# Convolution: sixteen of its 120 multiply-add taps made on the scalar engine and summed by accumulating DMA, two after each head norm

## The chip, the cores and the metric

The kernel runs on one NeuronCore of a Trainium2 chip. The metric is device time in microseconds (us) of that core. Five engines work side by side, each through its own instructions in order: PE (TensorE, matrix products), DVE (VectorE), ACT (ScalarE), POOL (GpSimd) and SP (SyncE, which here only issues DMAs). POOL also issues DMAs, among them those that add to their target while they write it ("accumulating" DMAs).

## What is computed

Two transformer-like blocks run on one sequence of 512 tokens with 1024 channels, all in float32. The change lies in the first half of the second block:

```python
proj = rms_norm(x, norm1_g) @ w_in
q, k, v, glu_a, glu_b = split(proj)            # 512 columns each
q = rms_norm(q per head of 64, q_norm_g);  k = rms_norm(k per head, k_norm_g)
attn = stick_breaking_attention(q, k, v)       # 8 heads, strictly causal
c = glu_a * sigmoid(glu_b)
c = causal_depthwise_conv(c, conv_dw_w, conv_dw_b)   # 31 taps, 512 channels
c = silu(layer_norm(c, conv_ln_g, conv_ln_b))
x = x + concat([attn, c]) @ w_out
```

The depthwise convolution is a sum over k of `w[k] * c[t - 30 + k]`, for each channel on its own. Everything else (the first block, the two feed-forward parts) stays as it is.

## The kernel before

Activations stand with channels in the partitions: a row of 512 channels is four chunks of 128 partitions x 512 tokens. A product in near-float32 is made of three PE passes (`mm3`, lines 127 to 129), each on a high or a low part of the operands; `copy_split` (L135, L136) and `scale_split` (L143, L144) make these parts, the high one on ACT and the low one on DVE.

Weights come in units of 1 MB through `prep`: SP loads `raw`, ACT casts it to `whi` (L199), and the low part `wlo` is made either by DVE (L205) or, for the eight units in `SUMMED`, by ACT writing minus the high part (L202) and POOL issuing an accumulating DMA that adds `raw` to it (L203). `raw`, `whi` and `wlo` have two buffers each.

The stage that matters runs so. `glu(i)` (four of them) makes chunk i of the gated input into `cc`. `heads` runs twice, for q and for k; for each of four token tiles it makes 24 PE products into one PSUM tile, squares it on ACT (L742), sums by head on DVE (L744), makes the reciprocal root on POOL in three small instructions (L745 to L747) and multiplies on DVE (L748, here called the head norm's last step). Then PE transposes the four tiles (L755, 16 products on the identity) and `scale_split` makes qT or kT. `project` makes v. The attention goes over twelve steps (hp, n) with hp 0 to 3 and n 0 to 2: `sticks` makes scores on PE (L785, L790), takes their absolute value on ACT for hp 0 and 1 (L794) and on DVE for hp 2 and 3 (L797), exp and ln on ACT (L799, L800), the sum on DVE (L801) and its two parts (L135, L136); `breaks` adds the tail sums on PE (L814, L817) and takes exp on ACT (L819); `gather` makes the weighted sum on PE (L829).

The convolution lies in between. `conv(n, after)` emits the next n taps of the list `TURNS`, each one DVE instruction `cv[:, i] += w[k] * cc[:, i, k:k+512]` (L851); the first tap of a chunk stands on an ACT instruction with scale and bias (L132). All 120 taps are chained by `issue_after`, so that they stay in order. When the last is done `conv_norm` makes the layer norm (L889 to L917). `attended` and `half_out` are the products with w_out.

A scheduler puts the emitted instructions into each engine's order by its own estimate of times; an engine then waits at each instruction for what that needs, and everything queued behind waits too.

Of the kernel before, what the change touches and what calls it, by code (L numbers as in the profile page):

```python
# [10 lines left out]
F32 = mybir.dt.float32  # L11
F32R = mybir.dt.float32r
I32 = mybir.dt.int32
AF = mybir.ActivationFunctionType
ALU = mybir.AluOpType
# [3 lines left out]
T = 512  # L19
# [60 lines left out]
def block_kernel(  # L80
# [12 lines left out]
    pe, act, dve, pool, sp = nc.tensor, nc.scalar, nc.vector, nc.gpsimd, nc.sync  # L93
# [78 lines left out]
    def half(name, a, b, dt=F32R):  # L172
        return part(slot(name, dt), a, b)
# [77 lines left out]
    def par(name, i=0, n=1):  # L251
        o = _SMALL[name][0] + i
        return sm[:, o : o + n]
# [119 lines left out]
    for u in range(2):  # L373
# [10 lines left out]
        sums = {}  # L384
# [307 lines left out]
    cc = part(ht[0], 4, 544)  # L692
    cv = part(ht[1], 4, T)
# [3 lines left out]
    def glu(i):  # L697
        pt = sta_unit(ph, pl)
        if i == 0:
            norms()  # L700
        ab = v3(t4(), 2, 512)
        dve.tensor_tensor(ab, pt, over2(rb2), ALU.mult)
        sig = act.activation(ab[:, 1, :], ab[:, 1, :], AF.Sigmoid)
        if i == 3:
            with tc.issue_after(sig.ins):
                act.preload_act_table_set(tables)
        return dve.tensor_tensor(cc[:, i, 30:542], ab[:, 0, :], ab[:, 1, :], ALU.mult)  # L707
# [18 lines left out]
    rr, rr2 = keep("rr"), keep("rr2")  # L726

    def heads(name, gain, sc, taps, between, early=()):

        gc = col(1)  # L730
        dve.tensor_scalar(gc, par(gain), sc, None, ALU.mult)
        ws = list(early) + [weights() for _ in range(2 - len(early))]
        dst = [half(name + "0", 4, T), half(name + "1", 4, T)]
        for t in range(NT):
            ps = single() if t < 2 else pair()[:, 0, :]
            st = slice(t * P, (t + 1) * P)
            for k in range(KC):
                wh, wl = (w[:, k % 4, :] for w in ws[k // 4])
                mm3(ps, ph[:, k, st], pl[:, k, st], wh, wl, k == 0, k == KC - 1)
            qn = norm2[:, t, :]  # L740
            heads8 = qn.rearrange("p (b d) -> p b d", d=HD)
            act.activation(qn, ps, AF.Square)  # L742
            ms = tp.tile([P, 8], F32, tag="col16", name="col16", bufs=6)
            dve.tensor_reduce(ms, heads8, AX.X, ALU.add)  # L744
            pool.tensor_scalar(ms, ms, rr2[:, t : t + 1], EPS, ALU.mult, ALU.add)  # L745
            pool.tensor_tensor(ms, ms, mhalf[:, :8], ALU.pow)  # L746
            pool.tensor_scalar(ms, ms, rr[:, t : t + 1], None, ALU.mult)  # L747
            conv(taps[t], dve.tensor_tensor(heads8, ps.rearrange("p (b d) -> p b d", d=HD),  # L748
                                            ms.unsqueeze(2).to_broadcast([P, 8, HD]), ALU.mult))
        between()  # L750
        for i in range(2):
            tr = pair().rearrange("p a (b c) -> p (a b) c", b=2)
            for t in range(2):
                for hp in range(4):
                    pe.transpose(tr[:, hp, t * P : (t + 1) * P],  # L755
                                 norm2[:, 2 * i + t, hp * P : (hp + 1) * P], ident)
            ts = slice(2 * i * P, (2 * i + 2) * P)
            scale_split(dst[0][:, :, ts], dst[1][:, :, ts], tr, gc)
        return dst
# [72 lines left out]

    TURNS = [0] * 8 + [0, 1] * 22 + [1, 2] * 8 + [2, 3] * 22 + [3] * 8
    done = [0] * 4
    tap = None

    def conv(n, after=None):

        nonlocal tap
        tap = after or tap
        for _ in range(min(n, len(TURNS))):
            i = TURNS.pop(0)
            k = done[i]
            done[i] += 1
            if k == 0:
                identity(cv[:, i, :], cc[:, i, 30:542], scale=par("dw_w", 4 * 30 + i),
                         bias=par("dw_b", i))
            with tc.issue_after(tap.ins) if tap else nullcontext():  # L850
                tap = dve.scalar_tensor_tensor(  # L851
                    cv[:, i, :], cc[:, i, k : k + 512], par("dw_w", 4 * k + i), cv[:, i, :],
                    ALU.mult, ALU.add)

    norm2 = half("D1", 4, T, F32)
    conv(8, glu(0))
    split_early(2)
    conv(16, glu(1))
    qT = heads("G", "qg", HD ** -0.5, (0, 4, 4, 8), lambda: conv(8, glu(2)), early[:2])
    kT = heads("F", "kg", 1.0, (0, 6, 5, 8), lambda: conv(12, glu(3)), early[2:])  # L860
    v2 = half("E0", 4, T, F32)
    stk = {}

    def place(i):
# [106 lines left out]
    seq = [(hp, n) for hp in range(4) for n in range(3)]  # L971
# [4 lines left out]
    todo = 2  # L976
    for i, x in enumerate(seq):

        while todo < len(seq) and todo <= i + 2 and not (x[1] == 2 and seq[todo][1] == 1):
            conv(2, sticks(*seq[todo]))  # L980
            todo += 1
        weighted = breaks(*x)
        if x[1] == 2:
            gathered = gather(x[0])
    with tc.issue_after(weighted.ins):
        act.preload_act_table_set("silu_and_others")
    assert not TURNS
    conv_norm()
# [127 lines left out]
```

## Time and profile before

| | us |
|---|---|
| median of 3 runs (lowest, highest) | 1244.39 (1243.74, 1244.77) |
| the profiled execution | 1245.94 |
| its span, first to last instruction | 1244.2 |
| mean granted TensorE clock in it | 0.995 of full |
| PE busy | 1230.3 (99%) |
| DVE busy | 754.0 (61%) |
| ACT busy | 495.0 (40%) |
| POOL busy | 113.5 (9%) |

Times below count from the first instruction of the profiled execution. Busy time of PE is modelled (products overlap), so that a busy PE is not always a PE at its peak; the distance from one product's start to the next's, and the waits, are the better measure. The second block starts near 665 us; the last attention product starts near 841 us.

### The profile page before, as it was taken

The page shows a single profiled execution, that of the slowest core. Times are in us where ns is not written, and L with a number is a line of the kernel's source. Part 1 is how long each engine was busy: PE and PEld are TensorE (multiplying, and loading weights), DVE is VectorE, ACT ScalarE, POOL GpSimd, SP SyncE. Part 2 cuts the span into 40 slices and gives each one's busy share as a digit, 9 for nine tenths or more (in the row PEclk, how much of TensorE's full clock was granted, in tenths as well). Part 3 has the DMA queues.
Part 4 walks back from the last instruction along what each step waited for, and adds up shares of the span by engine and source line. Part 5 has one row for each costly group of instructions (what it writes and reads, how often), then busy time and mean ns, then how long its engine had stood idle before and what let it go on. Part 6 is the DMA issues. An engine that isn't in the chain of part 4 may idle for free.

```text
span 1244.2 us, 13667 instructions
## 1 busy us (share of the span) xinstructions
PE 1230.3 (99%) x5712; PEld 1014.1 (82%) x5712; DVE 754.0 (61%) x823; ACT 495.0 (40%) x534; POOL 113.5 (9%) x137
## 2 busy tenths in 40 slices
PE   9999999999999999999999999999999999999998
PEld 7889888788888888888888887667888888888887
DVE  7855634744766674466373899877575555346532
ACT  6433424623544342243255338764343333123310
POOL 1100210012000000000053440000400000000000
PEclk9999999999999999999999999899999999999999
DMA  7223222312222222222346254301322222222222
GB/s 274 101 104 132 102 102 68 136 68 98 73 100 102 102 102 102 88 85 99 119 152 169 68 130 104 106 1 68 102 102 82 89 100 102 102 102 102 84 70 83
DMA packets 21597, 126.71 MB, mean 102 GB/s; under 512 B 2336, under 2 KB 4256, under 8 KB 7840
## 3 DMA queue, kind: packets, MB, share of 16 engines
q1 hardware_dynamic: 20096, 117.20, 26.7%
q0 software_dynamic: 1152, 8.39, 3.5%
q8 instruction: 44, 0.72, 0.2%
q10 hardware_dynamic: 288, 0.26, 0.1%
q14 instruction: 17, 0.14, 0.0%
HBM read 115.35 MB, written 2.10 MB: 94 GB/s over the span
## 4 chain that ended last, share of the span: by engine, by line
PE 90%; DVE 4%; POOL 2%; ACT 2%; issue 1%; DMA 1%; SPq 0%; DVEq 0%; POOLq 0%; ACTq 0%
PE pp L129 27%; PE pp L127 27%; PE pp L128 27%; DVE H L851 2%; PE ps L128 1%; PE ps L129 1%; PE ps L127 1%; POOL col L746 1%; PE pp L814 1%; PE pp L817 1%; PE ps L829 1%; DMA wlo<-raw 1%; POOL col L745 1%; PE pp L785 0%; PE ps L326 0%
## 5 line engine op out<-in xcount | busy, mean ns | idle before, releaser
L199 ACT CAST whi<-raw 128x2048 fp32r<-128x2048 f32 (+3 forms) x109 | 197.9, 1817 | 415.5 <-PE pp L128 335.7
L129 PE MATMUL pp<-B,wlo 128*128 128x512 f32 x672 | 262.5, 391 | 0.2
L127 PE MATMUL pp<-B,whi 128*128 128x512 f32 x672 | 261.7, 390 | 0.8 <-ACT whi L199 0.7
L128 PE MATMUL pp<-C,whi 128*128 128x512 f32 x672 | 262.2, 390 | 0.0
L205 DVE TENSOR_TENSOR wlo<-raw,whi 128x2048 fp32r<-128x2048 f32 (+3 forms) x101 | 219.3, 2172 | 66.1 <-ACT whi L199 65.6
L128 PE MATMUL pp<-G,whi 128*128 128x512 f32 x448 | 175.0, 391 | 0.0
L129 PE MATMUL pp<-F,wlo 128*128 128x512 f32 x416 | 162.2, 390 | 0.0
L127 PE MATMUL pp<-F,whi 128*128 128x512 f32 x416 | 161.5, 389 | 0.0
L129 PEld LDWEIGHTS pp<-B,wlo 128*128 128x128 f32 x672 | 126.1, 188 | 28.2 <-DVE wlo L205 1.5
L127 PEld LDWEIGHTS pp<-B,whi 128*128 128x128 f32 x672 | 126.3, 188 | 28.0 <-ACT whi L199 1.7
L128 PEld LDWEIGHTS pp<-C,whi 128*128 128x128 f32 x672 | 126.2, 188 | 26.8 <-issue 0.5
L128 PEld LDWEIGHTS pp<-G,whi 128*128 128x128 f32 x448 | 84.1, 188 | 17.5 <-issue 0.2
L655 DVE SCALAR_TENSOR_TENSOR H<-H,sm,H 128x512 f32<-128x512 f32 x132 | 92.8, 746 | 0.7
L634 DVE TENSOR_TENSOR A<-pp,A 128x1024 f32<-128x1024 f32 x23 | 28.2, 1224 | 105.5 <-PE pp L129 105.5
L129 PEld LDWEIGHTS pp<-F,wlo 128*128 128x128 f32 x416 | 78.1, 188 | 16.5 <-issue 0.2
L127 PEld LDWEIGHTS pp<-F,whi 128*128 128x128 f32 x416 | 78.1, 188 | 16.4 <-issue 0.2
L851 DVE SCALAR_TENSOR_TENSOR H<-H,sm,H 128x512 f32<-128x512 f32 x120 | 83.2, 742 | 2.7 <-ACT H L132 2.5
L660 DVE TENSOR_TENSOR H<-pp,rb 128x1024 f32<-128x1024 f32 x22 | 26.8, 1224 | 50.6 <-PE pp L129 44.4
L132 ACT ACTIVATE H<-H,sm 128x512 f32<-128x512 f32 x70 | 54.3, 808 | 4.6 <-DVE H L707 4.6
L1010 DVE TENSOR_TENSOR H<-pp,rb 128x512 f32<-128x512 f32 x22 | 15.2, 691 | 60.4 <-PE pp L129 55.3
L127 PE MATMUL pp<-D,whi 128*128 128x512 f32 x112 | 43.6, 389 | 0.0
L128 PE MATMUL pp<-E,whi 128*128 128x512 f32 x112 | 43.6, 389 | 0.0
(315 smaller groups left out, 1826.3 us busy)
## 6 DMA issues: line engine op xcount, KB each, us to landing
raw<-in_wts SPq DMA_DIRECT2D x99, 1024.0 KB, 4.8
wlo<-raw POOLq DMA_DIRECT2D x8, 1024.0 KB, 7.0
raw<-in_wts SPq DMA_DIRECT2D x8, 768.0 KB, 4.2
A<-in_xT SPq DMA_DIRECT2D x3, 512.0 KB, 6.7
out<-A SPq DMA_DIRECT2D x3, 512.0 KB, 2.8
D<-in_memT SPq DMA_DIRECT2D x1, 1024.0 KB, 11.4
raw<-in_wts SPq DMA_DIRECT2D x3, 256.0 KB, 7.6
A<-in_xT SPq DMA_DIRECT2D x2, 256.0 KB, 3.9
```

What stands on the lines that cost most here:

```text
L127: pe.matmul(out, wh, xh, start=start, stop=False, **kw)
L128: pe.matmul(out, wh, xl, start=False, stop=False, **kw)
L129: pe.matmul(out, wl, xh, start=False, stop=stop, **kw)
L132: act.activation(out, in_, AF.Identity, scale=scale, bias=bias)
L199: act.copy(hi[:, cs], raw[:, cs])
L205: dve.tensor_tensor(lo[:, cs], raw[:, cs], hi[:, cs].bitcast(F32), ALU.subtract)
L634: dve.tensor_tensor(hu, pt, hu, ALU.add)
L655: dve.scalar_tensor_tensor(dst, hs[:, k : k + 512], w(k), dst, ALU.mult, ALU.add)
L660: dve.tensor_tensor(hs[:, :, 2:], pt, over2(rb), ALU.mult)
L745: pool.tensor_scalar(ms, ms, rr2[:, t : t + 1], EPS, ALU.mult, ALU.add)
L851: tap = dve.scalar_tensor_tensor(cv[:, i, :], cc[:, i, k : k + 512], par("dw_w", 4 * k + i), cv[:, i, :], ALU.mult, ALU.add)
L1010: dve.tensor_tensor(hs[:, 2:514], pt[:, 0, :], rb, ALU.mult)
```

## The change

Taps 22 to 29 of chunks 0 and 1 leave `TURNS` (16 of 120). In their place `by_dma`, called once behind each of the eight head norms, makes two products `w[k] * cc[:, i, k:k+512]` on ACT (i = 0 and 1). For the first tap (k = 22) they are written straight into `sums[:, 0:2]`; for the other seven, into `sums[:, 2:4]`, from where POOL issues an accumulating DMA (256 KB) into `sums[:, 0:2]`, not before the last POOL instruction of that head norm (`power`, L747). That is 16 products and 14 DMAs. After the k heads one DVE instruction (128 x 1024) adds the sums to chunks 0 and 1 of `cv`. `sums` lies in the buffer D0, which the first attention step writes next. `TURNS` is reordered, and in the attention loop each step now emits one tap where it emitted two.

```diff
-            pool.tensor_scalar(ms, ms, rr[:, t : t + 1], None, ALU.mult)
+            power = pool.tensor_scalar(ms, ms, rr[:, t : t + 1], None, ALU.mult)
             conv(taps[t], dve.tensor_tensor(heads8, ps.rearrange("p (b d) -> p b d", d=HD),
                                             ms.unsqueeze(2).to_broadcast([P, 8, HD]), ALU.mult))
+            by_dma(power)
...
-    TURNS = [0] * 8 + [0, 1] * 22 + [1, 2] * 8 + [2, 3] * 22 + [3] * 8
+    TURNS = [0] * 8 + [0, 1] * 14 + [1] * 8 + [2] * 26 + [2, 3] * 4 + [3] * 26
...
+    sums = half("D0", 4, T, F32)
+    aside = list(range(22, 30))
+
+    def by_dma(behind):
+        k = aside.pop(0)
+        for i in range(2):
+            out = sums[:, i, :] if k == 22 else sums[:, 2 + i, :]
+            act.activation(out, cc[:, i, k : k + 512], AF.Copy, scale=par("dw_w", 4 * k + i))
+            if k > 22:
+                with tc.issue_after(behind.ins):
+                    pool.dma_start(out=sums[:, i, :], in_=out, accum_op=ALU.add)
+
     conv(8, glu(0))
...
     v2 = half("E0", 4, T, F32)
+    dve.tensor_tensor(cv[:, 0:2, :], cv[:, 0:2, :], sums[:, 0:2, :], ALU.add)
...
-            conv(2, sticks(*seq[todo]))
+            conv(1, sticks(*seq[todo]))
```

The scheduler's orders change with it, at three places above all. In each fence the words in brackets name the engines or DMA lanes that the instruction waits for (lanes of POOL's DMAs are DMASW, of SP's DMAHW).

POOL, from the third tile of the k heads to the fourth, before:

```order
L745 TENSOR_SCALAR col_4896<-col_4896,rr_4358 128x8 [waits DVE_49]
L746 TENSOR_TENSOR col_4896<-col_4896,mhalf 128x8 [waits Pool_49]
L747 TENSOR_SCALAR col_4896<-col_4896,rr 128x8 [waits Pool_49]
L203 DMA wlo<-raw 128x2048 [waits DMAHW3_49,DMASW2_49,Activation_49]
L745 TENSOR_SCALAR col_4933<-col_4933,rr_4358 128x8 [waits DVE_49]
L746 TENSOR_TENSOR col_4933<-col_4933,mhalf 128x8 [waits Pool_49]
L747 TENSOR_SCALAR col_4933<-col_4933,rr 128x8 [waits Pool_49]
```

and now:

```order
L868 DMA D_4360<-D_4360 128x512 [waits DMASW2_49,Activation_49]
L868 DMA D_4360<-D_4360 128x512 [waits DMASW3_49,Activation_49]
L745 TENSOR_SCALAR col_4919<-col_4919,rr_4358 128x8 [waits DVE_49]
L746 TENSOR_TENSOR col_4919<-col_4919,mhalf 128x8 [waits Pool_49]
L747 TENSOR_SCALAR col_4919<-col_4919,rr 128x8 [waits Pool_49]
L868 DMA D_4360<-D_4360 128x512 [waits DMASW4_49,Activation_49]
L868 DMA D_4360<-D_4360 128x512 [waits DMASW5_49,Activation_49]
L203 DMA wlo<-raw 128x2048 [waits DMAHW3_49,Activation_49]
L745 TENSOR_SCALAR col_4960<-col_4960,rr_4358 128x8 [waits DVE_49]
L746 TENSOR_TENSOR col_4960<-col_4960,mhalf 128x8 [waits Pool_49]
L747 TENSOR_SCALAR col_4960<-col_4960,rr 128x8 [waits Pool_49]
```

Two DMA issues, each waiting for an ACT product, now stand ahead of each head norm's three instructions, and ahead of the weight's DMA (L203).

ACT at the same place (L742 squares a tile, L202 and L199 prepare a unit of v's weights), before:

```order
L742 ACTIVATE D_4359<-pp 128x512 [waits PE_49]
L202 ACTIVATE wlo<-raw 128x2048 [waits DMAHW3_49,DMASW2_49,PE_49]
L742 ACTIVATE D_4359<-pp 128x512 [waits PE_49,Activation_49]
L199 CAST whi<-raw 128x2048
L199 CAST whi<-raw 128x2048 [waits DMAHW4_49,PE_49,Activation_49]
```

and now:

```order
L865 ACTIVATE D_4360<-H_2137,sm 128x512 [waits DMASW2_49,Activation_49]
L865 ACTIVATE D_4360<-H_2137,sm 128x512 [waits DMASW3_49,Activation_49]
L742 ACTIVATE D_4359<-pp 128x512 [waits PE_49]
L865 ACTIVATE D_4360<-H_2137,sm 128x512 [waits DMASW4_49,Activation_49]
L865 ACTIVATE D_4360<-H_2137,sm 128x512 [waits DMASW5_49,Activation_49]
L202 ACTIVATE wlo<-raw 128x2048 [waits DMAHW3_49,PE_49]
L742 ACTIVATE D_4359<-pp 128x512 [waits PE_49]
L199 CAST whi<-raw 128x2048
L865 ACTIVATE D_4360<-H_2137,sm 128x512 [waits DMASW6_49,Activation_49]
L865 ACTIVATE D_4360<-H_2137,sm 128x512 [waits DMASW7_49,Activation_49]
```

Each product waits until the DMA of the tap before has read and summed its buffer, and the squares of the head norm and the weight casts stand behind it in ACT's order.

PE, where the scores of the first attention steps (L785, L790) stand among v's products (the 128x512 rows onto `ps`; the first that reads the second unit's `wlo` is the last row shown), before:

```order
L785 MATMUL pp<-G_4552,F_4798 128x384 x2
L790 MATMUL pp<-never,identr 128x128 x2
L785 MATMUL pp<-G_4552,F_4798 128x256 x2
L785 MATMUL pp<-G_4552,F_4798 128x128 x2
L790 MATMUL pp<-never,identr 128x128 x4
L785 MATMUL pp<-G_4552,F_4797 128x512 x2
L785 MATMUL pp<-G_4553,F_4797 128x512 x2
L128 MATMUL ps_5124<-wlo,B_4163 128x512
```

and now:

```order
L786 MATMUL pp<-G_4553,F_4813 128x384 x2
L786 MATMUL pp<-G_4554,F_4813 128x384 x2
L786 MATMUL pp<-G_4553,F_4814 128x384 x2
L791 MATMUL pp<-never,identr 128x128 x2
L128 MATMUL ps_5156<-wlo,B_4163 128x512
```

Twelve score rows that stood ahead of that product now stand behind it. The last score rows of step (0, 2) now stand behind all of v's products, right ahead of the first tail sums:

```order
L128 MATMUL ps_5234<-wlo,B_4163 128x512
L129 MATMUL ps_5234<-whi,C_4165 128x512
L786 MATMUL pp<-G_4553,F_4814 128x512 x2
L791 MATMUL pp<-never,identr 128x128 x2
L815 MATMUL pp<-D_5098,negone 128x128 x2
```

Before, the same four rows stood 48 of v's products earlier, so that ACT could begin with step (0, 2) there. In the changed kernel DVE and PE also reach `conv_norm` inside the attention loop instead of behind it.

## Rows read from the trace of the kernel before

**Rows 1.** Busy time by stretch: us, then each engine's busy us, PEclk, DMA share, GB/s.
```profile
712.00:746.00 34.00, 34.00 (x159) 28.28 (x158) 32.27 (x48) 12.61 (x13) 15.56 (x14) 1.00 0.45 113
746.00:780.00 34.00, 33.87 (x179) 26.93 (x176) 33.97 (x47) 27.88 (x29) 2.65 (x3) 1.00 0.47 115
780.00:836.00 56.00, 50.27 (x300) 35.95 (x300) 44.10 (x56) 36.89 (x47) 0.00 (x0) 0.91 0.17 51
...
789.30:799.50 10.20, 9.34 (x45) 8.05 (x45) 7.70 (x9) 5.82 (x8) 0.00 (x0) 0.50 0.04 18
```

**Rows 2.** PE's longer waits from 780 to 862: total us, times, longest.
```profile
PE ps L829 <- ACT C L819: 1.5, 1, 1.5
PE ps L829 <- ACT E L819: 0.9, 1, 0.9
PE pp L785 <- ACT C L819: 0.9, 1, 0.9
PE pp L814 <- DVE t L801: 0.9, 1, 0.9
PE pp L814 <- DVE B L136: 0.7, 1, 0.7
PE pp L127 <- DVE A L957: 0.7, 1, 0.7
```

**Rows 3.** Timeline of DVE in the second attention step: start, us, instruction, idle before.
```profile
789.37 0.96 DVE L801 SCALAR_TENSOR_TENSOR t<-pp,t 128x768 f32<-128x768 f32 x1
```

**Rows 4.** Timeline of ACT just before it, same columns.
```profile
788.49 0.85 ACT L800 ACTIVATE t<-t 128x768 f32<-128x768 f32 x1
```

**Rows 5.** Timeline of DVE: eight taps in a row, and one 128x1024 step.
```profile
706.39 5.38 DVE L851 SCALAR_TENSOR_TENSOR H<-H,sm,H 128x512 f32<-128x512 f32 x8
...
746.52 1.21 DVE L702 TENSOR_TENSOR t<-pp,rb 128x1024 f32<-128x1024 f32 x1
```

**Rows 6.** Timeline of ACT: a 128x512 scaling, and a weight step in the k heads.
```profile
686.38 0.80 ACT L132 ACTIVATE H<-H,sm 128x512 f32<-128x512 f32 x1
...
733.64 1.92 ACT L202 ACTIVATE wlo<-raw 128x2048 fp32r<-128x2048 f32 x1 [4.62 <-PE pp L128]
```

**Rows 7.** Timeline of POOL: the fourth k tile's norm and two weight DMA issues.
```profile
735.86 0.93 POOL L203 DMA_DIRECT2D wlo<-raw  x1 [0.53 <-ACT wlo L202]
738.74 1.27 POOL L745 TENSOR_SCALAR col<-col,rr 128x8 f32<-128x8 f32 x1 [1.95 <-DVE col L744]
740.09 2.06 POOL L746 TENSOR_TENSOR col<-col,mhalf 128x8 f32<-128x8 f32 x1
742.25 0.31 POOL L747 TENSOR_SCALAR col<-col,rr 128x8 f32<-128x8 f32 x1
748.60 0.94 POOL L203 DMA_DIRECT2D wlo<-raw  x1 [6.04 <-ACT wlo L202]
```

**Rows 8.** Timeline of DVE: the last step of the fourth k tile's norm.
```profile
742.60 0.69 DVE L748 TENSOR_TENSOR D<-pp,col 128x512 f32<-128x512 f32 x1 [0.66 <-POOL col L747]
```

**Rows 9.** DMA queue of POOL (packets, MB, share), and issues (count, KB, us to landing).
```profile
q0 software_dynamic: 1152, 8.39, 3.5%
...
wlo<-raw POOLq DMA_DIRECT2D x8, 1024.0 KB, 7.0
...
A<-in_xT SPq DMA_DIRECT2D x2, 256.0 KB, 3.9
```

**Rows 10.** Timeline of PE: transposes of k, first scores, a product on v's second unit.
```profile
744.55 1.91 PE L755 MATMUL pp<-ident,D 128*128 128x128 f32 x16
...
746.53 0.40 PE L128 MATMUL ps<-wlo,B 128*128 128x512 f32 x1
...
752.30 1.26 PE L785 MATMUL pp<-G,F 64*128 64x256 f32 x14
...
755.68 0.50 PE L128 MATMUL ps<-wlo,B 128*128 128x512 f32 x1
```

**Rows 11.** Timeline of ACT: the absolute value of step (0, 2).
```profile
763.00 1.01 ACT L794 ACTIVATE t<-pp 128x1024 f32<-128x1024 f32 x1
```

## The prediction

> **What bounds the kernel now.** I read busy time by stretch first [rows 1]. From 712 to 780 us, where the heads of q and k and v's products run, PE is busy for 67.87 of 68 us: nothing that shortens DVE there shortens the kernel. DVE is as full (66.24 of 68), so it looks like a bottleneck, but nobody who ends the time waits for it. PE has idle time only in the attention loop: 5.73 of 56 us between 780 and 836. There the second view, PE's waits, says for whom [rows 2]: 1.6 us for DVE (L801 0.9, L136 0.7), the rest, 4.1 us, for ACT, above all for the exp (L819) between two PE products that depend on each other. One more wait for DVE (L957, 0.7) lies behind the loop. The third loss is the clock: from 789.3 to 799.5 PE was granted 0.50, the lower of its two levels (1.2 of 2.4 GHz), right behind the first cluster of waits. It was busy 9.34 us of that [rows 1], so at the full clock the same work takes 4.7 us less. All that a better convolution can win is thus about 1.6 + 0.7 us of waits for DVE and, if the waits go far enough, 4.7 us of clock.
>
> **What the taps cost.** Eight taps in a row take 5.38 us, start to start 0.66 [rows 5]; sixteen fewer free 10.6 us of DVE, and the one 128x1024 addition takes about 1.2 back (the same shape, L702, took 1.21 [rows 5]): 9.4 us net. On PE's path that is worth little. The wait for L801 ended at 789.37 + 0.96, and L801 started at 789.37, 0.03 us after the ln that it needs (788.49 + 0.85) [rows 3, 4]: the two taps ahead of it held it up by nothing. I leave 0 for the two waits in the loop and take the 0.7 of L957, since the layer norm's DVE work moves out of that place into the loop. Bounds: 0 and 2.3 us won. **Gain 0.7.**
>
> **What the products cost.** Sixteen at about 0.74 (the 128x512 scaling took 0.80 with its end [rows 6]) are 12 us of ACT, in a stretch where ACT is busy 12.61 of 34 us [rows 1]: room enough, as work. What counts is order: the squares (L742) and v's weight casts stand behind products that wait for a landing.
>
> **The landing** of a 256 KB accumulating DMA is not in the trace. The 1 MB ones land 7.0 us after their issue [rows 9]. Their queue shows 3.5% of 16 engines' 1244 us, 697 us for 8 DMAs: 5.4 us per engine and DMA. With a quarter of the bytes in as many packets this is 1.4 if bytes decide and 5.4 if packets do, so the landing lies between 1.6 + 1.4 = 3.0 and 7.0 us. A plain 256 KB load of the same shape took 3.9, in the crowded start [rows 9]. I take 3.2, near the end by bytes. The Trainium skill ("DMA: Bandwidth & Descriptors", section "Anatomy of one DMA — SWDGE (gpsimd) path") gives 2.0 us plus bytes over 436 GB/s, an estimate of 2.6 us here, and by it the sum below would be +2.6 instead of +3.0; but for 1 MB it gives 4.4 where the trace shows 7.0, so the trace decides.
>
> **POOL and the k heads.** An issue takes 0.93 and a norm 1.27 + 2.06 + 0.31 = 3.64 [rows 7], so a tile now costs POOL 2 x 0.93 + 3.64 = 5.5 us. PE makes a tile in the same time: 25 products lie between 746.53 and 752.30 [rows 10], 0.23 each, 24 to a tile. POOL can follow, but works off no lag. The first two products stand ahead of the first square and leave a lag of about 1.2; two issues add 1.86. So the weight issue (L203) behind the third k norm goes from 735.86 to about 738.9, the fourth norm ends near 739.9 + 3.64 = 743.5, and its last DVE step (L748, 0.69) near 744.3 instead of 743.3 [rows 7, 8]. The transposes start at 744.55, and those that need the fourth tile half of 1.91 later, at 745.4 [rows 10]: 1.1 us of lead are left. **Cost 0** at 3.2. If the landing is longer, each tile's chain is landing + 0.74, against 5.5: it is covered up to 4.7, and at 7.0 three tiles lose 2.2 each, 6.6 us, less the lead: 5.5 on PE. The q heads have more room, their second half of transposes moved nine products back.
>
> **v's weights.** The low part of v's first unit is now issued at about 738.9; with 7.0 us [rows 9] it lands at 745.9, and PE reads it at 746.53 [rows 10]; since small DMAs are still in flight on that queue I take a wait of 0.4. The second unit's issue stays near 748.60 [rows 7], because its cast waits for PE, not for the products; it lands at 755.6. Before, 28 score rows stood ahead of the product that reads it, and PE came to it at 755.68 [rows 10]. Now sixteen do, so that PE is there at about 752.30 + 28 rows' 3.4 us x 16/28 + 0.1 = 754.3 and waits until 755.6 to 756.3 (the next weight load now starts later and shares the engines), while the twelve rows are still to be done. **Cost 1.6**, bounds 1.0 and 2.5. Together 2.0. The addition on DVE waits for the last landing, near 748, and DVE reaches it near 749: cost 0; beyond that kT's low part, and with it the first scores, come late one for one.
>
> **The loop.** Step (0, 2) had its scores in time for ACT to begin at 763.00 [rows 11]. Now its last rows end behind v's products, at about 773, and ACT's weight casts stand ahead of it, so that its ln is ready only near 782 and its low part near 787. PE reaches its tail sums near 785. Walking the orders with the same durations I get waits of 1.1 (the scores of the next step, for the exp), 1.1, 1.2 and 0.5 (high and low parts) where the trace had 0.6, 0.7 and 0.9 [rows 2]: **cost 1.7**, bounds -1 and +4. Behind that DVE has six taps and the layer norm's 8 us where it had 17 taps, about as much; the exp waits stay what they are. I keep the clock's fall, at the same price.
>
> **The sum.** -0.7 + 0 + 2.0 + 1.7 = +3.0 us. The profiled execution of before took 1245.94, its span 1244.2 and 1.7 around it; it lies 1.55 above the median of the runs, 1244.39. The same change on the median gives **1247.4 us**.
>
> **Rivals.**
> - No measurable change: the second weight lands as PE comes (-1.2), and the loop's order costs no more than before (-1.3): 1244.9. For it speaks that PE's idle time in the loop is made of exp waits that any order has; against it, that 12 score rows really were the cover of that landing.
> - Faster: the relief of DVE does reach the loop. All 2.3 us of waits for DVE go [rows 2], the weights cost nothing: 1242.1; and if the cluster of waits at 786 to 790 gets short enough that the clock stays up, up to 4.7 less. For it speaks that DVE is the fullest engine beside PE in the loop (44.10 of 56 [rows 1]); against it, that L801 waited for ln and not for taps, and that (0, 2) comes later.
> - Much slower: the chain of landings decides, from a landing of 4.7 us on. At 7.0 the k transposes wait 5.5, which swallows the 2.0 of the weights: +6.5, 1250.9. The change then doesn't do what it says: a tap is not two products behind a head norm, but a head norm behind two landings.
> - Much slower by the clock: PE idles 1.5 to 2 us near 755, in a stretch that had no such gap, and the grant falls there once more: +4.7, 1252.1. In the trace one fall came behind waits of 0.6 and 0.7, and none behind the single one of 1.5 [rows 1, 2]. The Trainium skill ("TensorE: Matmul & The Clock Gate", "Part 1: The HAM clock gate (the "warmup" mystery)") says that the clock follows how busy PE has lately been and is throttled by default; the trace agrees as far as that one fall goes.
>
> **How the numbers follow.** Forecast (+1.5 to +4.5) 0.31; no measurable change 0.27; faster 0.22; landings 0.10; a second fall 0.10. A measurement of this kernel can tell about 0.2%, 2.5 us, from no change. Of the forecast's own spread a little lies under +2.5, which I put against what of the second rival lies above: faster 0.22, same 0.31, slower 0.47. The range leaves out about 0.1 on each side: from 1241.0, where the relief and part of the clock are won, to 1252.5, just beyond a second fall. The likeliest case alone has 1245.9 to 1248.9; cases of both signs hold the rest.
>
> **What would show it.** Right: 256 KB landings near 3.2 us; no PE wait at the k transposes; a wait of 1 to 2 us for `wlo` near 755; exp waits as long as before; one stretch of 0.50 clock behind 785. Wrong: landings beyond 4.7 with ACT's products waiting for them and PE for L748; a loop with less than 4 us of PE idle; no fall of the clock, or two. That DVE sheds 9.4 us of work without PE's time following is the core of it: if the time falls by more than 2.5 us, that step is wrong.

## The result: 9.5 us slower, and the profile after

| | us | |
|---|---|---|
| before, median | 1244.45 | 1243.74 to 1244.77 |
| after, median | 1253.99 | 1253.28 to 1254.34 |
| ratio | 1.0077 | 95% interval 1.0059 to 1.0094 |
| profiled execution, after (before) | 1254.34 (1245.94) | span 1251.8 (1244.2) |

The time lay 6.6 us above the prediction and 1.5 above its range, and the interval of the ratio leaves no doubt that it is slower. The same stretches as in [rows 1], now after the change, with the three falls of the clock behind them (us, busy us of PE, PEld, DVE, ACT, POOL with instructions, PEclk, DMA share, GB/s):

```profile
712.00:746.00 34.00, 33.65 (x159) 27.87 (x158) 28.85 (x41) 20.37 (x22) 22.90 (x24) 1.00 0.70 143
746.00:780.00 34.00, 30.16 (x135) 23.01 (x133) 30.23 (x40) 18.40 (x20) 2.56 (x3) 0.90 0.49 120
780.00:836.00 56.00, 50.37 (x305) 34.65 (x306) 47.39 (x61) 42.98 (x53) 2.54 (x2) 0.91 0.30 76
749.20:752.60 3.40, 3.40 (x9) 2.61 (x9) 2.70 (x4) 2.06 (x3) 0.08 (x1) 0.50 1.19 205
759.50:762.90 3.40, 2.99 (x7) 2.41 (x8) 3.25 (x5) 0.00 (x0) 0.00 (x0) 0.50 0.62 181
793.60:803.80 10.20, 10.09 (x35) 7.17 (x35) 8.19 (x12) 4.72 (x6) 0.00 (x0) 0.50 0.27 102
```

The loop has as much idle time as before (50.37 us of PE in 56, before 50.27). The loss lies ahead of it, where PE had been full: 4.2 us of PE idle from 712 to 780 instead of 0.13, and a mean clock of 0.90 from 746 to 780 instead of 1.00, which is 34 x 0.10 = 3.4 us. Together that is 7.5 us, where the span grew by 7.6. Two smaller differences partly cancel: from 836 to 870 PE idles 0.10 us instead of 0.65, and ahead of 640, where neither kernel has a product or a transfer of this change, it idles 0.9 more. PE's own waits from 640 to 780 (total, times, longest), and its timeline there (start, us, instruction, idle before and its releaser):

```profile
PE ps L128 <- DMA wlo<-raw: 3.8, 2, 2.0
PE pp L756 <- DVE D L748: 0.4, 1, 0.4
```
```profile
745.68 1.06 PE L756 MATMUL pp<-ident,D 128*128 128x128 f32 x8 [0.35 <-DVE D L748]
746.50 0.47 PE L127 MATMUL ps<-whi,B 128*128 128x512 f32 x1
748.97 0.60 PE L128 MATMUL ps<-wlo,B 128*128 128x512 f32 x1 [2.00 <-DMA wlo<-raw]
...
757.64 0.44 PE L791 MATMUL pp<-never,identr 128*128 128x128 f32 x2
759.91 0.80 PE L128 MATMUL ps<-wlo,B 128*128 128x512 f32 x1 [1.83 <-DMA wlo<-raw]
```

Both waits are for v's weights (low parts), and each is followed by a stretch at 0.50. Why the first is late is read on ACT and POOL, from the second k tile on:

```profile
722.72 0.60 ACT L742 ACTIVATE D<-ps 128x512 f32<-128x512 f32 x1 [1.16 <-PE ps L129]
730.88 0.72 ACT L865 ACTIVATE D<-H,sm 128x512 f32<-128x512 f32 x1 [7.57 <-DMA D<-D]
732.66 0.72 ACT L865 ACTIVATE D<-H,sm 128x512 f32<-128x512 f32 x1 [1.05 <-DMA D<-D]
733.29 0.58 ACT L742 ACTIVATE D<-pp 128x512 f32<-128x512 f32 x1
735.94 0.72 ACT L865 ACTIVATE D<-H,sm 128x512 f32<-128x512 f32 x1 [2.07 <-DMA D<-D]
737.24 0.73 ACT L865 ACTIVATE D<-H,sm 128x512 f32<-128x512 f32 x1 [0.57 <-DMA D<-D]
737.87 1.90 ACT L202 ACTIVATE wlo<-raw 128x2048 fp32r<-128x2048 f32 x1
```
```profile
727.38 1.84 POOL L868 DMA_DIRECT2D D<-D  x2 [0.17 <-issue]
...
738.79 1.85 POOL L868 DMA_DIRECT2D D<-D  x2
740.06 1.46 POOL L203 DMA_DIRECT2D wlo<-raw  x1
...
748.42 0.86 POOL L203 DMA_DIRECT2D wlo<-raw  x1 [1.59 <-ACT wlo L202]
```

ACT stood for 7.57 us at a product (L865) that waits for the transfer of the pair before; that transfer was issued only at 727.38, behind the first k tile's norm on POOL. The square of the third tile (L742) stood behind the product: 733.29, where before it started at 728.42. The weight's low cast (L202) comes at 737.87, before at 733.64 [rows 6], and its issue at 740.06, before at 735.86 [rows 7]. Landings, from issue to arrival: of the whole kernel (count, KB, median us), then of v's two weights (7.0 for each before); 8.9 is the first and 11.4 the second:

```profile
wlo<-raw POOLq DMA_DIRECT2D x8, 1024.0 KB, 7.8
...
D<-D POOLq DMA_DIRECT2D x14, 256.0 KB, 3.8
```
```profile
DMA to landing us min/median/max: 8.9/10.2/11.4
```

### The profile page after: what moved, and what is told of

The parts are those of the page before. It is cut to its first block, busy times and chain, and to the rows that moved or that the text cites. A ratio compares the mean times of both kernels' runs of the same rounds, so it can differ in the third digit from the quotient of the medians.

```text
span 1251.8 us, 13703 instructions
## 1 busy us (share of the span) xinstructions
PE 1233.6 (99%) x5712; PEld 1013.5 (81%) x5712; DVE 749.1 (60%) x808; ACT 505.8 (40%) x550; POOL 126.4 (10%) x151
## 4 chain that ended last, share of the span: by engine, by line
PE 87%; DVE 4%; ACT 3%; DMA 2%; POOL 2%; issue 1%; SPq 0%; DVEq 0%; ACTq 0%; POOLq 0%
PE pp L129 27%; PE pp L128 27%; PE pp L127 27%; PE ps L128 1%; PE ps L127 1%; PE ps L129 1%; DMA D<-D 1%; DMA wlo<-raw 1%; POOL col L746 1%; ACT whi L199 1%; DVE H L852 1%; PE pp L818 1%; DVE t L802 0%; POOL col L745 0%; DMA A<-in_xT 0%
## 5 line engine op out<-in xcount | busy, mean ns | idle before, releaser
L199 ACT CAST whi<-raw 128x2048 fp32r<-128x2048 f32 (+3 forms) x109 | 197.9, 1817 | 403.5 <-PE pp L128 328.0
L205 DVE TENSOR_TENSOR wlo<-raw,whi 128x2048 fp32r<-128x2048 f32 (+3 forms) x101 | 219.4, 2173 | 66.2 <-ACT whi L199 65.7
L655 DVE SCALAR_TENSOR_TENSOR H<-H,sm,H 128x512 f32<-128x512 f32 x132 | 92.8, 747 | 0.7
L852 DVE SCALAR_TENSOR_TENSOR H<-H,sm,H 128x512 f32<-128x512 f32 x104 | 75.7, 747 | 4.1 <-ACT H L132 2.5
```

Source lines behind the costliest of these rows:

```text
L199: act.copy(hi[:, cs], raw[:, cs])
L205: dve.tensor_tensor(lo[:, cs], raw[:, cs], hi[:, cs].bitcast(F32), ALU.subtract)
L655: dve.scalar_tensor_tensor(dst, hs[:, k : k + 512], w(k), dst, ALU.mult, ALU.add)
L852: tap = dve.scalar_tensor_tensor(cv[:, i, :], cc[:, i, k : k + 512], par("dw_w", 4 * k + i), cv[:, i, :], ALU.mult, ALU.add)
```

## Experiments

Ratios are to runs of the kernel before on the same chip, with 95% intervals; its median there was 1245.1 to 1245.6. Line numbers shift by a few between kernels. The theories: **A** the transfers cost the time by way of v's weights; **B** the products and the addition; **C** PE's new order; **D** the relief of DVE is large and eaten up; the others come with the runs. e1, e2, e5, e6, e9 and e13 leave taps or parts of them out of the sum; all others compute all of it.

### The change taken apart

**e1** leaves out the transfers:
```
-                    pool.dma_start(out=sums[:, i, :], in_=out, accum_op=ALU.add)
```


> The changed kernel with its fourteen accumulating transfers left out; the sixteen products on the scalar engine, the shorter table of taps and the addition stay (seven taps of two chunks are missing from the sum). Theory A (the transfers cost the time: they delay v's weights on POOL's queue, PE waits, and the clock falls behind the waits): no product waits for a landing, the first v weight is issued within 1 us of 735.9, no PE wait for wlo between 740 and 762, no clock fall before 785, and the time is 1242.5 to 1245.5. Rival B (the products on ACT and the addition on DVE cost it): ACT's weight casts stay late and the time stays above 1249. Rival C (the new order of PE's rows costs it): with the twelve score rows back ahead of the second weight, as this build orders them, the time is near 1246 to 1248, the first wait of about 2 us stays.

1248.49, ratio 1.0030 (1.0018 to 1.0042). No PE wait from 740 to 762 and one clock fall, so A holds there, and products and addition by themselves (B) do not cost that time. Without transfers the addition waits for no landing, though; its wait is part of A. The expected 1242.5 to 1245.5 did not come: new waits appeared behind the loop.

```profile
843.74 0.96 PE L127 MATMUL pp<-G,whi 128*128 128x512 f32 x3 [1.37 <-ACT G L135]
...
852.73 0.50 PE L127 MATMUL pp<-G,whi 128*128 128x512 f32 x1 [2.53 <-DVE A L969]
```

With fewer taps the layer norm comes earlier. Its four Silu (840.29 to 843.2 on ACT) now stand ahead of the cast of the last G, and its low parts ahead of L969 on DVE; both are what PE needs next.

**e2** takes the relief alone: `by_dma(power)` and the addition are removed, the short table stays.

> The changed kernel without products, transfers and addition: sixteen taps are just left out of the sum, so DVE keeps the whole relief of 10.6 us at no price. PE keeps the changed kernel's order at the second weight of v, with sixteen score rows ahead of it. The prediction's step (the relief is worth about 0.7 us, bounds 0 and 2.3): 1242 to 1244. Theory A adds: the second v weight lands near 755.6 as before while PE comes to it near 754, a wait of 1 to 1.6 us, and one clock fall behind it would cost 1.7 more, so 1244 to 1247. Rival D (the relief reaches the loop, and only the chain eats it): below 1241.

1254.45, ratio 1.0075 (1.0063 to 1.0087). This ended every simple account, mine too: 10.6 us less work on DVE, nothing added, and 9 us slower. PE waits 1.74 us for the second v weight, right behind which the clock falls, and the waits of 1.4 and 2.5 behind the loop are there. A third loss is in the loop, where PE waits three times for a low part on DVE:

```profile
755.49 0.50 PE L128 MATMUL ps<-wlo,B 128*128 128x512 f32 x1 [1.74 <-DMA wlo<-raw]
```
```profile
PE pp L817 <- DVE C L136: 4.0, 3, 1.9
```

**e3** takes the price alone: table and `conv(2, ...)` of before, products and transfers kept, no addition.

> All 120 taps stay on DVE in the order of before, and products and transfers run beside them into a tile that nobody adds: the price without the relief. PE has the order of before at the second weight of v (28 score rows ahead). Theory A: the first v weight is late as in the changed kernel (a PE wait of about 2 us near 747 and a clock fall of about 3.4 us behind it), the second wait shrinks to about 0.5 by the twelve rows, so 1249 to 1252. Rival C (PE's order costs the time): 1244 to 1246. Rival D (the relief is worth several us in the changed kernel): above 1256.

1252.21, ratio 1.0057 (1.0045 to 1.0069). The waits for the weights are both there (1.63 and 2.27 us), although 28 score rows stand ahead of the second one. So the second wait has two causes, each enough: PE's order (e2) and the transfers (e3). The two prices, 8.8 and 6.6 us, do not add up in the whole change (9.5). In part they share the second wait; in part e2's losses (4.0 in the loop, 3.9 behind it, the clock at 0.50 near 825 and 862) do not occur in the changed kernel, whose waits ahead of the loop are like those of e3.

**e4** computes v's low parts on DVE (`SUMMED` without the two).

> The changed kernel with the low parts of v's two weights computed by a subtraction on DVE (two of 128x2048, some 2 us each) instead of a transfer on POOL's queue; the products' transfers stay where they are. Theory A: both PE waits for wlo (3.8 us together) and the two clock falls behind them (1.7 us each) go, less what 4 us more on DVE cost, so 1245 to 1248. Rival B or C (products, addition or order cost the time): 1251 or more. If the chain of landings held up the k heads themselves, a PE wait for L748 above 1 us shows.

1252.92, ratio 1.0061 (1.0048 to 1.0074): hardly a gain, and above the 1245 to 1248 that A gave. The first wait goes, the second becomes one for L205 on DVE (1.84 at 754.94), and the waits of e1 behind the loop come.

### The order that a shorter DVE brings

In the kernel before ACT makes both halves of kT's high parts in a row. In e2 and in the changed kernel (below) the last gate's sigmoid (L703) and the load of ACT's next function table stand between them. The likely reason is that with less on DVE the scheduler expects the gate's input earlier; its estimates are in no run, the order that it chose is.

```profile
748.03 1.09 ACT L143 ACTIVATE F<-pp,col 128x1024 fp32r<-128x1024 f32 x1
750.51 0.63 ACT L703 ACTIVATE t<-t 128x512 f32<-128x512 f32 x1 [1.38 <-DVE t L702]
751.16 1.28 ACT L706 ACT_TABLE_LOAD   x1
752.45 1.12 ACT L143 ACTIVATE F<-pp,col 128x1024 fp32r<-128x1024 f32 x1
```

The twelve score rows that need the second half of k then go behind v's second weight: these were the cover of its landing. **e5** is e2 with the order of before forced, **e6** adds one for the Silu:

```
+            with tc.issue_after(state["high"].ins) if i == 3 else nullcontext():   # e5: kT's high part
                 sig = act.activation(ab[:, 1, :], ab[:, 1, :], AF.Sigmoid)
...
-            with tc.issue_after(weighted.ins):
+            with tc.issue_after(gathered.ins):                      # e6: a DVE instruction
                 act.activation(ci, ci, AF.Silu, ...)
```


> The run e2 (sixteen taps left out of the sum, no products, no transfers, no addition) with one order forced: the sigmoid and table load of the last gate are issued behind the second half of kT's high parts on ACT, as in the kernel before; in e2 and in the changed kernel they stand between the two halves, and PE's rows for the second half of k move behind v's products. Theory E (this order costs e2 its time): PE has 28 score rows ahead of the second v weight again, no PE wait for wlo, no clock fall near 756, time 1246.5 to 1249 (the waits of 1.4 and 2.5 us behind the attention loop stay, as in e1). Rival F (having fewer taps costs the time in the loop, whatever the order ahead of it): 1252 or more.

> e5 with a second order forced: the four Silu of the layer norm are issued behind the low part of the last attention output G, so that ACT's cast of G does not stand behind them. Theory E: the waits of 1.4 us for G and of 2.5 us for DVE behind the loop shrink to about 0.7 together, so 1242 to 1245: this is the most that the relief can bring, 0 to 3 us less than before. Rival F: 1250 or more. Rival G (DVE's queue behind the loop is full in any order): the wait of 2.5 stays and the time is 1246 to 1248.

e5: 1248.54, ratio 1.0026 (1.0016 to 1.0037), 5.9 us less than e2 by that one order: the wait for the second weight, the 4.0 us in the loop and all falls of the clock but the loop's one are gone. e6 (1255.74, ratio 1.0082, 1.0069 to 1.0095) failed as an experiment: an order behind an instruction of another engine did not hold ACT's queue, so that Silu and exp alternate, with seven more table loads than e9 below (not eight, as its expectation says), each of 1.28 us:

```profile
821.42 1.28 ACT L936 ACT_TABLE_LOAD   x1
822.71 0.81 ACT L936 ACTIVATE H<-H,sm 128x512 f32<-128x512 f32 x1
823.54 1.28 ACT L804 ACT_TABLE_LOAD   x1
```

**e9** holds the Silu behind ACT's own cast of the last G.

> e6 done right: there nothing held the Silu behind the exps on ACT, and eight more table loads came of it; here the four Silu are issued behind ACT's own cast of the last G. Sixteen taps are left out of the sum, no products, no transfers. Theory E: the wait of 1.3 us for G behind the loop goes and the 2.5 us for DVE shrinks to under 0.5, the loop keeps the 2.8 us less PE idle that e1 and e5 show; with the clock's fall near 789 as before 1242 to 1244.5, the most that the relief can bring. Rival G (the relief is worth nothing in any order): 1245 to 1248.

1242.53, ratio 0.9986 (0.9978 to 0.9995). Here is the relief: PE is busy 53.15 of 56 us in the loop (before 50.27), and 33.12 of 34 behind it (before 33.35). It is worth 2.6 us by the medians, 1.7 by the ratio (0.6 to 2.7).

### The chain of transfers in the k heads

**e7** is the changed kernel with the gate's order of e5. **e10** is the changed kernel with the products of k's last two tiles issued behind the cast of v's first weight. **e11** has e10, the gate and the Silu.

```
-            by_dma(power)                                           # e10
+            if name == "G" or t < 2: by_dma(power)
+            else: powers.append(power)
...
+    for power in powers: by_dma(power, state[65])     # state[65]: ACT's low cast of v's first unit
```


> The changed kernel with the first of the two orders forced (the last gate's sigmoid behind kT's high parts), its products and transfers untouched. Theory A+E (two causes, each enough for the wait at the second v weight): the first wait of about 2 us for wlo and the clock fall behind it stay, the second shrinks at best to 0.5 as the chain still delays that weight's landing, so 1249 to 1253, like e3. If the order alone made the changed kernel slow: 1245 to 1248.

> The changed kernel with one order changed: the products of k's last two tiles are issued on ACT behind the cast of the first v weight's low part, so that POOL issues that weight's transfer ahead of them (near 736 as before, not 740.06). The gate's order stays as in the changed kernel. Theory A: the first PE wait for wlo (2.0 us) and the fall of the clock behind it (3.4 us at half, 1.7 us lost) go; the second wait stays at 1.5 to 2.5: 1249 to 1252. Rival H (the landing is late because the queue's engines are full with the small transfers, whatever the order of issue): the first wait stays above 1 us and the time at 1253 to 1255.

> The changed kernel, all of it computed, with the three orders repaired: first v weight ahead of the products of k's last two tiles, last gate behind kT's high parts, Silu behind the cast of G. Theory A+E: no wait at the first v weight, 28 rows ahead of the second, which still lands late if the next weight load shares the engines with it (a wait of 0 to 1.5): 1243.5 to 1248. If the chain costs time by other ways: 1250 or more.

e7: 1256.12, ratio 1.0087 (1.0069 to 1.0106), worse than expected: the first wait for wlo is left (1.8), but the waits of 1.3 and 2.5 behind the loop come in. e10: 1252.59 (1.0059, 1.0046 to 1.0072), just above the expected 1249 to 1252. The weight is issued at 738.74, right behind the third norm on POOL and ahead of the pair of transfers (not near 736 as expected). The first wait shrinks from 2.00 to 0.43 as A said, and both weights now land in 7.0 us. But the chain is only pushed on, on to kT:

```profile
745.93 0.50 PE L128 MATMUL ps<-wlo,B 128*128 128x512 f32 x1 [0.43 <-DMA wlo<-raw]
...
757.39 0.68 PE L789 MATMUL pp<-G,F 64*128 64x256 f32 x8 [3.41 <-ACT F L143]
```
```profile
747.33 0.72 ACT L870 ACTIVATE D<-H,sm 128x512 f32<-128x512 f32 x1 [7.12 <-DMA D<-D]
```

e11: 1251.62 (1.0050, 1.0037 to 1.0063), again 4.1 us of PE waits at kT. Of these 2.7 are for kT's low part on DVE, and there the addition stands ahead of it and waits for the last landing:

```profile
755.22 1.23 DVE L889 TENSOR_TENSOR H<-H,D 128x1024 f32<-128x1024 f32 x1 [3.81 <-DMA D<-D]
...
757.81 1.28 DVE L144 SCALAR_TENSOR_TENSOR F<-pp,col,F 128x1024 fp32r<-128x1024 f32 x1
```
```profile
759.15 1.33 PE L793 MATMUL pp<-G,F 64*128 64x384 f32 x6 [2.69 <-DVE F L144]
```

With all orders but the chain's repaired, products, transfers and addition still cost 9.1 us over e9.

**e13** is e11 with half the columns in each transfer. **e14** takes eight taps of one chunk and three buffers, with the orders for gate and Silu. **e15** has these two orders too, and issues each pair behind the next tile's square on ACT, the last one behind kT's high parts; it also moves the addition on DVE from ahead of the first scores to behind them:

```
+            in_=out[:, :256]                                        # e13
+        out = sums[:, 0, :] if k == 22 else sums[:, 1 + k % 3, :]   # e14: one chunk, 8 taps
             square = act.activation(qn, ps, AF.Square)              # e15
+            if powers: by_dma(powers.pop(), square)
...
-            by_dma(power)
+            powers.append(power)
...
+    by_dma(powers.pop(), state["high"])                             # the last pair
-    dve.tensor_tensor(cv[:, 0:2, :], cv[:, 0:2, :], sums[:, 0:2, :], ALU.add)
...
     conv(14, sticks(*seq[1]))
+    dve.tensor_tensor(cv[:, 0:2, :], cv[:, 0:2, :], sums[:, 0:2, :], ALU.add)
```


> e11 (all three orders repaired) with each accumulating transfer cut to half its columns, 128x256 and 128 KB; the other half of the seven taps' products is not added. Products, issues and waits are as many as in e11. Theory I (the landing itself is the length of the chain behind the k tiles): landings fall from 3.8 to between 2.5 and 3.3, ACT's waits for them shrink by more than half, and the time falls by 3 us or more, to 1244 to 1248.5. Rival J (the chain is too long by its issues and its order in POOL's and ACT's queues, the bytes hardly matter): 1250 or more.

> Another split, all of the sum computed: eight taps of one chunk only, one product and one transfer behind each of the eight tiles' norms, with three product buffers instead of one for each chunk, and the gate and Silu orders of e9. Half the transfers, and ACT never waits for a landing. Theory I: no PE wait for wlo or kT between 740 and 762, v's first weight issued before 737.5, and half of the relief's 2.6 us: 1243 to 1245, as e12. Rival J: POOL's issues alone (0.93 each in the norm's queue) make the weight and the fourth norm late: 1246 or more.

> Sixteen taps as in the changed kernel, all of the sum computed, with the gate and Silu orders, but each pair of products is issued behind the next tile's square on ACT (and the addition behind the first scores), so that the square of a tile no longer stands behind a landing of the pair before it. If ACT's queue order (squares behind products that wait) makes the k norms late: the last k norm ends near 743 again, v's first weight is issued before 737.5, and the time is 1244 to 1248. If POOL's queue carries the same wait on (a transfer waits there for its product, and the next norm behind it): 1250 or more.

e13: 1245.98 (1.0014, 1.0004 to 1.0024), 5.6 us less than e11. The median landing fell only from 3.9 to 3.4, above the 2.5 to 3.3 expected, and ACT's waits for landings from 27.9 to 21.2 us, not by half; DVE's wait at the addition fell from 3.8 to 0.6. So the chain is sensitive to its length, but bytes are a small part of it. e14: 1249.23 (1.0038, 1.0024 to 1.0052), a miss: with three buffers ACT ran ahead and then waited all the same (18.8 us, longest 7.4), and the square of the third tile started at 731.75. e15: 1245.28 (1.0008, 0.9996 to 1.0021), all sixteen taps, no transfer less, and 8.7 us under the changed kernel. Its squares are on time (before: 728.42 and 735.46):

```profile
727.36 0.73 ACT L873 ACTIVATE D<-H,sm 128x512 f32<-128x512 f32 x1 [3.21 <-DMA D<-D]
728.38 0.60 ACT L746 ACTIVATE D<-pp 128x512 f32<-128x512 f32 x1 [0.29 <-PE pp L129]
...
736.08 0.57 ACT L746 ACTIVATE D<-pp 128x512 f32<-128x512 f32 x1
```

The rest of what I expected of e15 did not come. The last k tile's norm is as late as in the changed kernel (its last step on DVE starts at 744.64, there 744.84, before 742.60), and POOL's queue now stands for the products: 0.57 and 1.50 us at the second tile's two transfers. The weight is issued at 737.82, not before 737.5. But its cast on ACT starts at 734.27 instead of 737.87 and its issue stands ahead of the third tile's pair, so that both of v's weights land in 7.2 us and PE waits for neither:

```profile
734.27 1.90 ACT L202 ACTIVATE wlo<-raw 128x2048 fp32r<-128x2048 f32 x1
...
737.82 0.94 POOL L203 DMA_DIRECT2D wlo<-raw  x1
...
744.64 0.69 DVE L754 TENSOR_TENSOR D<-pp,col 128x512 f32<-128x512 f32 x1 [0.39 <-POOL col L753]
```

So the transfers as such need not cost the time; what stood behind them in the queues did, above all v's weights. How much of the 6.3 us from e11 to e15 is the order on ACT and how much the place of the addition stays open: no run moves one without the other. **e18** is the lag (with the moved addition) alone, without forced orders for gate and Silu.

> The changed kernel with the lag of e15 alone (each pair of products behind the next tile's square, the addition behind the first scores), without the orders forced for the gate and the Silu. Its build puts the gate behind kT's high parts and 28 score rows ahead of the second v weight by itself, but leaves the Silu ahead of the cast of G. If each cause counts by itself: the 740 to 764 losses go as in e15, the waits of 1.3 and 2.5 us behind the loop come as in e1 and e5, so 1247 to 1249.

1249.49 (1.0047, 1.0028 to 1.0066): as e15 up to 836, and the waits of 1.4 and 2.5 behind the loop are back. By the medians the lag gives 4.5 us over the changed kernel, and the forced orders 4.2 more; as the gate stands right in e18 by itself, that is the Silu's.

### Fewer taps, and a version that beats both

**e8** and **e12** take four taps (22 to 25) of each of the two chunks, behind the q tiles only and nothing behind the k tiles, with the gate's order and the Silu of e6 and of e9.

> Half the dose in the place where it is free, with both orders forced: taps 22 to 25 as products and transfers behind the four q tiles' norms only, nothing behind the k tiles; eight taps fewer on DVE than before, all of the sum computed. Theory A+E: v's weights are issued as before (735.9 and 748.6), no PE wait for wlo, one clock fall near 789 or none: 1242 to 1245.5. If the transfers behind q hurt as well (k's second weight late, issued at 716.8 in the changed kernel where before had 714.15): a PE wait for wlo near 720 to 726 and 1247 or more.

> e8 with the Silu held behind ACT's cast of G rather than left free. Theory E: the same 1243 to 1246 as e8, since in e8 the layer norm comes late enough that the Silu stand behind the exps anyway. A candidate to beat the kernel before: the ratio to it below 0.998 would show it.

1245.30 (1.0004, 0.9995 to 1.0013) and 1244.73 (0.9999, 0.9989 to 1.0008): free behind q, and worth nothing that can be measured.

**e16** and **e17** are e15 with fewer taps offered ahead of kT's low parts on DVE (in e15 PE waited twice 0.69 us for those).

```
-    kT = heads("F", "kg", 1.0, (0, 6, 5, 8), ...)       # then conv(12, ...)
+    kT = heads("F", "kg", 1.0, (0, 6, 2, 2), ...)       # e16: conv(21, ...)
+    kT = heads("F", "kg", 1.0, (0, 4, 2, 2), ...)       # e17: conv(23, ...)
```


> A version that might beat both kernels: e15 with fewer taps offered behind k's last two tiles (2 and 2 instead of 5 and 8, the rest later), so that no tap stands between the last gate's product (L702) and kT's low parts on DVE; all of the sum computed. In e15 PE waited twice 0.7 us for those low parts (752.4 and 754.3, in e9 749.7 and 751.6) and the clock fell for 3.4 us behind them. If the waits and that fall go: 1.4 + 1.7 less than e15, near 1242.5, that is at what the relief alone gives (e9). If not: 1244 to 1246.

> As e16 with two taps fewer again behind the tile before (4, 2, 2), by which the addition stands eight taps behind the last gate's output on DVE instead of three, and waits less for the last landing (1.3 us in e15). If DVE's wait for the landing reaches PE: 0.5 to 1 us less than e16. If it is covered: the same as e16 within 0.7 us.

e16: 1244.95 (0.9998, 0.9989 to 1.0007). The waits for kT are gone, but the addition reached DVE too early and held its queue, which came out in the loop:

```profile
DVE H L1000 <- DMA D<-D: 3.9, 1, 3.9
```

e17: **1243.36, ratio 0.9983 (0.9974 to 0.9992)**, 2.1 us under the kernel before and 10.6 under the changed one, all of the sum computed; DVE waits 0.4 us for that landing. The same two stretches as above:

```profile
746.00:780.00 34.00, 33.90 (x176) 26.85 (x174) 31.52 (x40) 28.94 (x31) 4.38 (x5) 1.00 0.66 157
780.00:836.00 56.00, 53.32 (x315) 37.89 (x314) 47.51 (x61) 36.68 (x47) 1.03 (x1) 0.91 0.17 50
```

The addition must not come much later: the tile of the sums becomes the first step's score tile.

## Why the prediction was wrong, point by point

- **What bounds the kernel: right.** PE's waits decide; sixteen taps less are worth 1.7 to 2.6 us (e9), against a bound of 2.3. That DVE sheds work without PE's time following was the core, and it held. The value 0.7 was low, and the loop, not L957, is where it comes.
- **The failed steps, in the sum's own terms: v's weights (2.0 forecast, 3.8 measured) and the clock, which had no term of its own ("I keep the clock's fall, at the same price") and cost 3.4.** The next points take them apart.
- **v's first weight: a wait of 0.4 forecast, 2.00 measured.** I had the issue at 738.9, which counts one pair of issues on POOL. A second pair stands between the third norm and the weight (two starts 0.63 apart, from 738.79), so it came at 740.06; ACT's cast, late by the third square, had ended only at 739.77. And I took a landing of 7.0 and measured 8.9, with two small transfers ahead on the queue; issued ahead of them, in e10, it took 7.0. Behind this wait came the first fall of the clock.
- **v's second weight: 1.6 forecast, 1.83 measured, by chance.** PE came 3.8 us later than forecast (758.08 for 754.3), and the landing took 11.4 us instead of 7.0. The next weight load from memory starts when the first v weight has landed, 748.98 instead of 742.88, and so ran beside it, as did the last pair of transfers (landed by 751.7). "Shares the engines" was in the text, but priced at 0.7 at most.
- **The clock: the rival that happened.** My forecast had a wait of 1.6 near 755 and a rival "PE idles 1.5 to 2 us near 755", after which the clock falls again, at 0.10. The forecast met the rival's condition, so they were one case, not two. The fall came twice and shorter: 3.4 us at half each, some 1.7 us lost in each, not 4.7. Whether it comes is not settled by the length of one wait. It came close behind the waits ahead of the loop in e2, e3, e4, e10 and e11, but not behind the 1.79 in e7 (749.36; the clock fell only at 758.8). The wait of 2.5 behind the loop had a fall behind it in e2, e4 and e7, none in e1, e5 and e18; two waits of 0.69 at kT had one in e15, none in e18. The Trainium skill ("TensorE: Matmul & The Clock Gate", "Part 1: The HAM clock gate (the "warmup" mystery)") says that the clock follows PE's recent activity. These rows agree in so far as every fall named here stands behind idle time of PE.
- **The relief costs nothing: missed altogether.** I took the orders of the other engines as given but for PE's 28 and 16 rows, which I saw without asking what moved them. It was ACT's order, the gate between the halves of kT (e5: 5.9 us in e2). A table of taps is also a table of everything that the scheduler then places earlier.
- **The landing: 3.8 measured for 3.2 forecast.** Size near, between the bounds, and under the 4.7 up to which I called it covered. The Trainium skill's figure for it ("DMA: Bandwidth & Descriptors", section "Anatomy of one DMA — SWDGE (gpsimd) path"), an estimate of 2.6, was further off.
- **"Each tile's chain is landing + 0.74, against 5.5": the mechanism was wrong, the time near by luck.** I set landing and product beside POOL's 5.5 us for a tile. They are one behind the other: transfer, product on ACT, then the square that stands behind it on ACT, the reduction, the norm, and only then the next transfer. The third square was 4.9 us late with a landing that the prediction called covered. Yet POOL's lag as I had it (1.2 + 1.86) moves the third norm from 731.50 to 734.56, and it started at 734.69. What I lost by pricing POOL alone was ACT's queue: the casts of v's weights stand there too.
- **k transposes: 0 forecast, 0.35 measured** (L748 at 744.84 for 744.3).
- **The loop: +1.7 forecast, -0.1 measured** (50.37 of 56 for 50.27), and the 0.7 of L957 did go: PE idles 0.55 less from 836 to 870. Of the waits cited there, the 0.6 is for ACT (L814 on L135) and not among the lines of [rows 2].

Sum as forecast: -0.7 + 0 + 2.0 + 1.7 = +3.0. Sum as measured in the trace: -0.55 for the gain, 0.35 for the transposes, 3.8 for the weights, 3.4 for the clock and -0.1 for the loop, 6.9 in all. With the 0.9 ahead of 640 that is 7.8, where the span grew by 7.6.

The medians differ by 9.5 us and the two spans by 7.6. Of the 1.9 between, 1.1 is where the profiled executions lay over their medians (1.5 before, 0.35 after); the other 0.8 lies outside the spans, and its cause stays open.

## What to carry to other kernels

A product that waits for a transfer holds everything behind it on its engine: write down, for each such wait, what stands next in that queue, and put the work on the path ahead of it (issuing the products one tile later, and the addition with them, was worth 4.5 us alone, e18, and 6.3 with the other orders held, e11 to e15). Count every issue that stands ahead of it, too: one pair was forgotten here. When an engine off the path gets less work, compare the orders of all engines before costing the relief at nothing: whatever the scheduler now places earlier may stand in front of what the path needs. And if the forecast's own wait fulfils a rival's condition, price both together.

## What the runs showed of the hardware

- Accumulating transfers from tile to tile on the core landed (median) in 3.4 us for 128 KB (e13), 3.8 for 256 KB and 7.0 for 1 MB undisturbed: as an estimate worked out from these three, about 3 us of each do not depend on its size.
- In the changed kernel a 1 MB one beside a 1 MB load (and, at first, two of 256 KB) landed in 11.4 us instead of 7.0, and that load in 11.1; the same load before, alone, took 4.8.
- Issued behind two of 256 KB on POOL's queue, a 1 MB one landed in 8.9 us (changed kernel), issued ahead of them in 7.0 (e10) and 7.2 (e15).
- Each change between the tables of exp and Silu cost 1.28 us on ACT; e6 had seven more of them than e9 and was 13 us above it.
